# Weight parts and FFN activations in slots 4160 bytes apart instead of 4096

## The chip, the cores and the metric

The kernel runs on one core of a Trainium2 chip. The metric is the device time of one execution in microseconds (us). TensorE (PE, with its weight loads shown as PEld), VectorE (DVE), ScalarE (ACT), GpSimd (POOL) and SyncE (SP, which issues the DMAs) run side by side and wait for each other through semaphores.

## The reference

Two layers of a decoder trunk over 512 tokens of width 1024. Each layer has three sublayers, and each ends in a residual sum and a layer norm:

```python
for l in range(2):
    h = layer_norm(ALPHA * h + 0.5 * swiglu(h, ffn1_in[l], ffn1_out[l]), ...)   # D_FF = 2816
    mix = hybrid_mixer(h, ...)   # h @ w_in -> pooling, sparse attention, S5 -> @ w_out
    h = layer_norm(ALPHA * h + mix, ...)
    h = layer_norm(ALPHA * h + 0.5 * swiglu(h, ffn2_in[l], ffn2_out[l]), ...)

def swiglu(x, w_in, w_out):
    gate, up = jnp.split(x @ w_in, 2, axis=-1)
    return (jax.nn.silu(gate) * up) @ w_out
```

Four FFNs (two in each layer) hold most of the work; the two mixers stand between them.

## The kernel before

**Numbers in two parts.** A float32 operand of the large products is cut into a high part (`hi`, rounded to fp32r by ACT, L100) and a low part (`lo`, the rest, made by DVE, L101). A product is then three fp32r matmuls into the same PSUM bank: high by high, high by low and low by high (`mm3`, L247 to L249, and `project`, L395).

**Weights as units.** All weights stream from HBM as units of 128 partitions by 1024 float32 (4096 bytes in a partition), in the order in which PE wants them (`weight_units`). `Weights.load` issues the DMA of a unit into one of three staging slots `st`; `Weights.prep` takes the next unit, makes its parts `wh` and `wl` and issues further loads. The parts have six slots each in the pool `wsplit`; `done` gives slots back and `pump` fills them again. PE works through its units in a fixed order, ACT, DVE and SP work ahead of it.

**An FFN.** In the first half 44 units are used as the stationary operand: for each of 8 pieces `k` of the contraction PE loads 128 columns of `wh` or `wl` and streams 512 columns of `xh` or `xl`, the parts of the transposed input (names `g` and `u` in rows; `hd` for the first four units, which are done in two halves of 256 tokens). Silu and the product with `u` go to tiles `a`, two to a slot of the pool `act` (13 slots, tag `u`). In the second half 22 units are the moving operand: PE loads 128 columns of the activation's parts `ap` (in the same `act` slots) and streams 512 columns of `wh` or `wl` (name `o`, L395). The last four units of this half are put into `act` slots instead of `wsplit` (`W.alt`), so that all tokens of one tile can be finished together while the norm starts (`tail_and_head`).

**A mixer.** Its input projection streams weights past 128-token pieces of `xh` and `xl` (names `a`, `b`, `c`, `s`; of the `c` units a piece is 280 columns, or 1120 bytes, wide). Its output projection is like an FFN's second half, with `xh` and `xl` as stationary operand; its last four units (89 to 92 in the first layer) go to a pool `tail` of eight slots at the upper end of SBUF.

Each matmul of these lines has a weight load of its own. While one matmul runs, the load of the next one is under way.

Of the kernel before, what the change touches and what calls it, by code (L numbers as in the profile page):

```python
# [7 lines left out]
F32 = mybir.dt.float32  # L8
F32R = mybir.dt.float32r
# [20 lines left out]
PI2_A = 6.28125  # L30
PI2_B = 0.0019340515136718750
PI2_C = 1.2556659146363256e-06
CH = 4
NCH = SEQ // CH

# [20 lines left out]
class Weights:  # L56
# [23 lines left out]
    def prep(self):  # L80
        nc, i = self.nc, self.n_ready
        ap, n, raw = self.units[i]
        if raw:
            self.load(i + 6)
            t = self.split.tile([128, 1024], F32, tag="wh", name=f"wh{i}")
            nc.sync.dma_start(t[:, :n], ap)
            self.live.add(i)
            self.ready[i] = t
            self.n_ready += 1
            return  # L90
        self.load(i + 1)
        t = self.loaded.pop(i)
        if i in self.alt:
            pool, th, tl = self.alt[i], "u", "u"
        else:
            pool, th, tl = self.split, "wh", "wl"
            self.live.add(i)
        hi = pool.tile([128, 1024], F32R, tag=th, name=f"wh{i}")
        lo = pool.tile([128, 1024], F32R, tag=tl, name=f"wl{i}")
        nc.scalar.activation(hi[:, :n], t[:, :n], AF.Copy)  # L100
        nc.vector.tensor_tensor(lo[:, :n], t[:, :n], hi[:, :n].bitcast(F32), op=ALU.subtract)  # L101
        self.ready[i] = (hi, lo)
        self.n_ready += 1
        self.load(i + 4)
# [22 lines left out]
class Trunk:  # L127
# [65 lines left out]
    def start(self):  # L193

        nc, io, W = self.nc, self.io, self.W
        st = [W.stage.tile([128, 1024], F32, tag="st", name=f"st{u}") for u in range(2)]
        hi = [W.split.tile([128, 1024], F32R, tag="wh", name=f"wh{u}") for u in range(2)]
        lo = [W.split.tile([128, 1024], F32R, tag="wl", name=f"wl{u}") for u in range(2)]

        def parts(h, l, src):  # L200
            nc.scalar.activation(h, src, AF.Copy)  # L201
            nc.vector.tensor_tensor(l, src, h.bitcast(F32), op=ALU.subtract)  # L202

        with self.tc.tile_pool(name="x_in", bufs=8) as xp:
            warm = xp.tile([128, SEQ], mybir.dt.bfloat16, name="warm", bufs=1)
            nc.vector.memset(warm, 0.0)
            ps = self.bank("warm")
            for _ in range(WARM):
                nc.tensor.matmul(ps, lhsT=warm[:, :128], rhs=warm, start=True, stop=True)
            ts = [xp.tile([128, SEQ], F32, tag="xt", name=f"xt{k}") for k in range(KD)]  # L210

            def piece(u, c, run):
                if run:
                    parts(hi[u][:, c], lo[u][:, c], st[u][:, c])
                else:
                    nc.sync.dma_start(st[u][:, c], W.units[u][0][:, c])

            def column(k, run):
                if run:
                    parts(self.xh[:, k], self.xl[:, k], ts[k])  # L220
                else:
                    nc.sync.dma_start(ts[k], io["xT"][k])

            a, b = slice(0, 256), slice(256, 1024)
            for run in (False, True):
                piece(0, a, run)
                column(0, run)
                piece(1, a, run)
                column(1, run)
                piece(0, b, run)  # L230
                column(2, run)
                piece(1, b, run)
                for k in range(3, KD):
                    column(k, run)
                if not run:
                    W.n_loaded = 2
                    W.load(3)
        for u in range(2):
            W.ready[u] = (hi[u], lo[u])
            W.live.add(u)  # L240
        W.n_ready = 2
        nc.gpsimd.memset(self.expo, -0.5)
        nc.gpsimd.memset(self.bd, 0.0)

    def mm3(self, out, ah, al, bh, bl, start, stop):
        mm = self.nc.tensor.matmul
        mm(out, lhsT=ah, rhs=bh, start=start, stop=False)  # L247
        mm(out, lhsT=ah, rhs=bl, start=False, stop=False)  # L248
        mm(out, lhsT=al, rhs=bh, start=False, stop=stop)  # L249
# [258 lines left out]
    def s5_matrices(self, l, ap):  # L508
# [13 lines left out]
        def cmul(outr, outi, xr, xi, yr, yi, t):  # L522
            po.tensor_tensor(outr, xr, yr, op=ALU.mult)
            po.tensor_tensor(t, xi, yi, op=ALU.mult)
            po.tensor_tensor(outr, outr, t, op=ALU.subtract)
            po.tensor_tensor(outi, xr, yi, op=ALU.mult)
            po.tensor_tensor(t, xi, yr, op=ALU.mult)
            po.tensor_tensor(outi, outi, t, op=ALU.add)
# [8 lines left out]
        def wide(a):  # L537
            return a.unsqueeze(2).unsqueeze(3).to_broadcast([128, 8, 2, 16])
# [6 lines left out]
        def sub(m, s):  # L545
            return m.rearrange("p j (g s c) -> p j g s c", g=2, s=CH)[:, :, :, s]

        for s in range(CH - 1):
            k = CH - 1 - s
            cmul(sub(ebr, s), sub(ebi, s), br, bi, wide(prm[f"a{k}r"]), wide(prm[f"a{k}i"]), t)  # L550
        po.tensor_copy(sub(ebr, CH - 1), br)
        po.tensor_copy(sub(ebi, CH - 1), bi)
        cmul(fcr, fci, cr, ci, wide(prm["fr"]), wide(prm["fi"]), t)
# [47 lines left out]
    def s5_params(self, ap):  # L601
# [16 lines left out]
        def ts(a, s1, op0, s2=None, op1=None, out=None):  # L618
            out = tmp() if out is None else out
            if op1 is None:  # L620
                ve.tensor_scalar(out, a, s1, None, op0=op0)
            else:
                ve.tensor_scalar(out, a, s1, s2, op0=op0, op1=op1)
            return out

        def stt(a, s, b, op0, op1, out=None):
            out = tmp() if out is None else out
            ve.scalar_tensor_tensor(out, a, s, b, op0=op0, op1=op1)
            return out
# [12 lines left out]
        r = stt(n, -PI2_B, r, ALU.mult, ALU.add)  # L642
        r = stt(n, -PI2_C, r, ALU.mult, ALU.add)
        r = ts(r, 3.1415925, ALU.min, -3.1415925, ALU.max)
# [782 lines left out]
```

## Time and profile before

| | |
|---|---|
| median of 3 runs (lowest, highest) | 1978.22 us (1977.77, 1979.16) |
| the profiled execution, its own time | 1978.67 us |
| its span in the trace | 1976.9 us |
| PE busy | 1959.7 us, 99% of the span |
| DVE, ACT, POOL busy | 47%, 33%, 15% of the span |

The span runs from the first to the last instruction; 1.8 us of the execution's own time lie around it. A matmul's row shows its start and its length with the way through the array (0.39 us for 512 columns). Successive matmuls overlap, so the rate is read from the distance between starts, called a step here: first start to last start of a stretch, divided by the number of matmuls between them.

### The profile page before, as it was taken

To read this page: it belongs to the slowest core of one execution; us is meant where nothing else is said; L and a number is where in the kernel's file an instruction comes from. 1 tells how busy PE (TensorE), PEld (TensorE's weight loads), DVE (VectorE), ACT (ScalarE), POOL (GpSimd) and SP (SyncE) were. 2 spreads that over 40 slices of the span, in tenths; PEclk is the share of its full clock that TensorE was granted. 3 is DMA by queue.
4 is the path that set the end of the run, shared out by engine and by line. 5 is a ranking of instruction groups with operands and counts; after the bars stand their busy time and mean duration, and the time that the engine had idled before them with its cause. 6 is when DMAs were issued, how large, how long until landed. Compare 5 with 4: busy or idle time off the path is not lost.

```text
span 1976.9 us, 24780 instructions
## 1 busy us (share of the span) xinstructions
PE 1959.7 (99%) x9940; PEld 1643.0 (83%) x9940; DVE 920.4 (47%) x1434; ACT 648.4 (33%) x1144; POOL 288.5 (15%) x399
## 2 busy tenths in 40 slices
PE   9999999999999999999999999999999999999998
PEld 7888888898788888888898888888977898888886
DVE  5322333657976323233643223346779662223335
ACT  4222233135861222233222222331358622222320
POOL 1804000113321000000044220001223210000001
PEclk9999999999999999999999999999999999999999
DMA  8333334022111333334233333340211213223331
GB/s 286 111 95 90 105 97 139 20 79 75 54 64 66 117 96 96 96 96 127 76 113 101 92 96 96 96 139 9 90 64 44 87 63 107 96 96 96 96 96 43
DMA packets 57186, 183.21 MB, mean 93 GB/s; under 512 B 11248, under 2 KB 12016, under 8 KB 57072
## 3 DMA queue, kind: packets, MB, share of 16 engines
q1 hardware_dynamic: 57072, 181.64, 29.1%
q8 instruction: 78, 1.28, 0.3%
q14 instruction: 36, 0.29, 0.1%
HBM read 179.19 MB, written 2.10 MB: 92 GB/s over the span
## 4 chain that ended last, share of the span: by engine, by line
PE 95%; DVE 3%; ACT 1%; DMA 1%; issue 0%; POOL 0%; SPq 0%; DVEq 0%; ACTq 0%
PE o L395 28%; PE g L247 8%; PE g L248 8%; PE g L249 8%; PE u L247 8%; PE u L249 7%; PE u L248 7%; PE o L1079 2%; PE pt L1063 2%; PE hd L247 1%; PE hd L249 1%; PE hd L248 1%; PE hid L751 1%; PE tx L318 1%; PE s L1027 1%; PE s L248 1%
## 5 line engine op out<-in xcount | busy, mean ns | idle before, releaser
L101 DVE TENSOR_TENSOR wl<-st,wh 128x1024 fp32r<-128x1024 f32 x308 | 379.3, 1236 | 596.3 <-ACT wh L100 581.3
L100 ACT ACTIVATE wh<-st 128x1024 fp32r<-128x1024 f32 x308 | 323.8, 1055 | 923.2 <-PE g L248 351.8
L395 PE MATMUL o<-wh,ap 128*128 128x512 f32 x1408 | 379.2, 389 | 0.0
L395 PEld LDWEIGHTS o<-wh,ap 128*128 128x128 f32 x1408 | 263.8, 188 | 54.4
L247 PE MATMUL g<-xh,wh 128*128 128x512 f32 x656 | 256.7, 391 | 0.7 <-ACT xh L201 0.7
L248 PE MATMUL g<-xl,wh 128*128 128x512 f32 x656 | 255.6, 390 | 0.8 <-DVE xl L202 0.8
L249 PE MATMUL g<-xh,wl 128*128 128x512 f32 x656 | 255.4, 389 | 0.0
L247 PE MATMUL u<-xh,wh 128*128 128x512 f32 x656 | 255.2, 389 | 0.0
L248 PE MATMUL u<-xl,wh 128*128 128x512 f32 x656 | 255.2, 389 | 0.0
L249 PE MATMUL u<-xh,wl 128*128 128x512 f32 x656 | 255.2, 389 | 0.0
L395 PE MATMUL o<-wl,ap 128*128 128x512 f32 x704 | 217.4, 389 | 0.0
L287 POOL TENSOR_TENSOR mv<-mv,expo 128x1 f32<-128x1 f32 x24 | 35.6, 1485 | 1191.3 <-DVE mv L286 1191.3
L430 DVE TENSOR_TENSOR a<-a,u 128x512 f32<-128x512 f32 x82 | 56.4, 688 | 257.3 <-PE u L249 257.3
L395 PEld LDWEIGHTS o<-wl,ap 128*128 128x128 f32 x704 | 132.1, 188 | 27.6
L247 PEld LDWEIGHTS g<-xh,wh 128*128 128x128 f32 x656 | 123.2, 188 | 27.5 <-ACT xh L201 2.5
L248 PEld LDWEIGHTS g<-xl,wh 128*128 128x128 f32 x656 | 123.2, 188 | 26.8 <-DVE xl L202 1.7
L249 PEld LDWEIGHTS u<-xh,wl 128*128 128x128 f32 x656 | 123.2, 188 | 25.7
L249 PEld LDWEIGHTS g<-xh,wl 128*128 128x128 f32 x656 | 123.1, 188 | 25.7
L247 PEld LDWEIGHTS u<-xh,wh 128*128 128x128 f32 x656 | 123.1, 188 | 25.5
L248 PEld LDWEIGHTS u<-xl,wh 128*128 128x128 f32 x656 | 123.1, 188 | 25.6
L475 DVE TENSOR_TENSOR ap<-a,ap 128x512 fp32r<-128x512 f32 x88 | 60.3, 689 | 70.3 <-ACT ap L474 70.3
L474 ACT ACTIVATE ap<-a 128x512 fp32r<-128x512 f32 x88 | 54.5, 624 | 97.1 <-PE o L395 61.5
(348 smaller groups left out, 2604.1 us busy)
## 6 DMA issues: line engine op xcount, KB each, us to landing
st<-in_ffn_in SPq DMA_DIRECT2D x174, 512.0 KB, 3.5
st<-in_ffn_out SPq DMA_DIRECT2D x88, 512.0 KB, 3.5
st<-in_w_out SPq DMA_DIRECT2D x16, 512.0 KB, 3.5
st<-in_w_b SPq DMA_DIRECT2D x8, 512.0 KB, 4.3
st<-in_w_a SPq DMA_DIRECT2D x8, 512.0 KB, 3.6
ln_g<-in_ln_g SPq DMA_DIRECT2D x6, 512.0 KB, 4.0
ln_b<-in_ln_b SPq DMA_DIRECT2D x6, 512.0 KB, 5.0
xt<-in_xT SPq DMA_DIRECT2D x8, 256.0 KB, 6.5
```

Source lines behind the costliest of these rows:

```text
L100: nc.scalar.activation(hi[:, :n], t[:, :n], AF.Copy)
L101: nc.vector.tensor_tensor(lo[:, :n], t[:, :n], hi[:, :n].bitcast(F32), op=ALU.subtract)
L247: mm(out, lhsT=ah, rhs=bh, start=start, stop=False)
L248: mm(out, lhsT=ah, rhs=bl, start=False, stop=False)
L249: mm(out, lhsT=al, rhs=bh, start=False, stop=stop)
L287: nc.gpsimd.tensor_tensor(mv[:, 2:3], mv[:, 2:3], self.expo, op=ALU.pow)
L395: mm(ps[t][f], lhsT=a[:, q], rhs=w[:, 512 * f:512 * f + 512], start=(k == first and a is ah and w is wh), stop=end)
L430: nc.vector.tensor_tensor(a, a, u, op=ALU.mult)
L474: nc.scalar.activation(p[:, 0], a, AF.Copy)
L475: nc.vector.tensor_tensor(p[:, 1], a, p[:, 0].bitcast(F32), op=ALU.subtract)
L1063: nc.tensor.transpose(ps[:, 128 * k:128 * k + 128], p[:, i, 128 * k:128 * k + 128], ident)
L1079: mm(o[64 * i:64 * i + 64], lhsT=self.v[:, b, k, 64 * g:64 * g + 64], rhs=pt[:, i, 128 * k:128 * k + 128], start=False, stop=b == 1 and k ...
```

## The change

The tiles of the weights' parts are declared 1040 columns wide, of which the first 1024 are used. A slot of the pool is as wide as its widest tile, so all slots of tag `u` in `act` (with the activations `a` and their parts `ap`) and in `tail` grow too. No instruction is added, taken out or moved.

```diff
+W_SLOT = 1040
@@ Weights.prep
-            t = self.split.tile([128, 1024], F32, tag="wh", name=f"wh{i}")
+            t = self.split.tile([128, W_SLOT], F32, tag="wh", name=f"wh{i}")[:, :1024]
...
-        hi = pool.tile([128, 1024], F32R, tag=th, name=f"wh{i}")
-        lo = pool.tile([128, 1024], F32R, tag=tl, name=f"wl{i}")
+        hi = pool.tile([128, W_SLOT], F32R, tag=th, name=f"wh{i}")[:, :1024]
+        lo = pool.tile([128, W_SLOT], F32R, tag=tl, name=f"wl{i}")[:, :1024]
@@ Trunk.start
-        hi = [W.split.tile([128, 1024], F32R, tag="wh", name=f"wh{u}") for u in range(2)]
-        lo = [W.split.tile([128, 1024], F32R, tag="wl", name=f"wl{u}") for u in range(2)]
+        hi = [W.split.tile([128, W_SLOT], F32R, tag="wh", name=f"wh{u}")[:, :1024] for u in range(2)]
+        lo = [W.split.tile([128, W_SLOT], F32R, tag="wl", name=f"wl{u}")[:, :1024] for u in range(2)]
```

Where the slots lie in a partition, in bytes, as the built programs place them:

| slots | before: first, step | remainder modulo 512 | after: first, step | remainders modulo 512 |
|---|---|---|---|---|
| `xh`, `xl`, staging `st` | 17664, 34048, 61696 | 256 | the same | 256 |
| `wh`, six | 73984, 4096 | 256 | 73984, 4160 | 256, 320, 384, 448, 0, 64 |
| `wl`, six | 98560, 4096 | 256 | 98944, 4160 | 128, 192, 256, 320, 384, 448 |
| `act`, thirteen | 125184, 4096 | 256 | 125952, 4160 | 0, 64, 128 and so on, all eight |
| `tail` of the mixers, eight | 196576, 4096 | 480 | 196064, 4160 | 480, 32, 96 and so on, all odd multiples of 32 |

A piece of 128 or 512 columns inside a unit starts at a multiple of 512 bytes from the slot's start, so it has the slot's remainder. The program has 7872 matmuls on lines L247 to L249 and L395. In 7415 of the 7871 pairs of neighbours, before, the moving operand of one and the weights of the next (which are loaded meanwhile) start at the same remainder; after, in 1165 pairs, and the rest is spread over the other multiples of 64, with some 600 to 1100 pairs for each.

The order of the instructions is the same on every engine. Since pools are larger, some tiles lie over other earlier tiles than before, and seven instructions wait for other semaphores. On DVE, these are the subtractions that make the low parts of the mixer's last units in the first layer (89 to 92) and of the next FFN's first (93); before:

```order
L1085 TENSOR_TENSOR xl_74<-o221_4671,xh_73 128x4x128 [waits Activation_49]
L101 TENSOR_TENSOR wl89_4922<-st89_4489,wh89_4921 128x1024 [waits DMAHW7_49,Activation_49]
L101 TENSOR_TENSOR wl90_4928<-st90_4532,wh90_4927 128x1024 [waits DMAHW0_49,Activation_49]
L101 TENSOR_TENSOR wl91_4958<-st91_4574,wh91_4957 128x1024 [waits DMAHW1_49,Activation_49,Pool_49]
L101 TENSOR_TENSOR wl92_4964<-st92_4925,wh92_4963 128x1024 [waits DMAHW5_49,Activation_49]
L101 TENSOR_TENSOR wl93_4994<-st93_4931,wh93_4993 128x1024 [waits DMAHW6_49,Activation_49]
```

and with the change:

```order
L1086 TENSOR_TENSOR xl_74<-o221_4671,xh_73 128x4x128 [waits Activation_49]
L102 TENSOR_TENSOR wl89_4922<-st89_4489,wh89_4921 128x1024 [waits DMAHW7_49,Activation_49]
L102 TENSOR_TENSOR wl90_4928<-st90_4532,wh90_4927 128x1024 [waits DMAHW0_49,Activation_49,Pool_49]
L102 TENSOR_TENSOR wl91_4958<-st91_4574,wh91_4957 128x1024 [waits DVE_49,DMAHW1_49,Activation_49,Pool_49]
L102 TENSOR_TENSOR wl92_4964<-st92_4925,wh92_4963 128x1024 [waits DMAHW5_49,Activation_49]
L102 TENSOR_TENSOR wl93_4994<-st93_4931,wh93_4993 128x1024 [waits DMAHW6_49,Activation_49]
```

The rows and their order are the same (line numbers are one higher); units 90 and 91 wait for POOL and DVE, whose last writes of the attention's tiles lay where the slots now lie. The same two units of the second layer, and ACT's `wh` of unit 91 and its twin, change in this way too, and a copy to `tabc` on POOL in the second layer loses its waits.

## Rows read from the trace of the kernel before

**Rows 1.** The page: span, busy time and share of each engine, granted clock in 40 slices

```profile
span 1976.9 us, 24780 instructions
PE 1959.7 (99%) x9940; PEld 1643.0 (83%) x9940; DVE 920.4 (47%) x1434; ACT 648.4 (33%) x1144; POOL 288.5 (15%) x399
PEclk9999999999999999999999999999999999999999
```

**Rows 2.** The page: the chain that ended last, by engine

```profile
PE 95%; DVE 3%; ACT 1%; DMA 1%; issue 0%; POOL 0%; SPq 0%; DVEq 0%; ACTq 0%
```

**Rows 3.** The chain of waits, 253 to 368 us: start us, us, what

```profile
252.97 114.24 PE o L395 x504
```

**Rows 4.** Timeline of PE, an FFN's first half: start us, us, instruction

```profile
199.76 0.39 PE L247 MATMUL g<-xh,wh 128*128 128x512 f32 x1
...
204.52 0.39 PE L247 MATMUL u<-xh,wh 128*128 128x512 f32 x1
```

**Rows 5.** Timeline of PE, matmuls of 256 columns

```profile
623.78 0.28 PE L247 MATMUL hd<-xh,wh 128*128 128x256 f32 x1
...
626.18 0.28 PE L249 MATMUL hd<-xh,wl 128*128 128x256 f32 x1
```

**Rows 6.** Timeline of PE where the granted clock is low

```profile
1442.11 0.63 PE L247 MATMUL a<-wh,xh 128*128 128x512 f32 x1
...
1444.24 0.63 PE L249 MATMUL a<-wh,xl 128*128 128x512 f32 x1
```

**Rows 7.** Two stages: us, busy us of PE, PEld, DVE, ACT, POOL, clock, DMA

```profile
598.93:615.73 16.80, 16.80 (x73) 13.48 (x72) 11.42 (x17) 1.06 (x1) 3.06 (x2) 1.00 0.14 45
1442.11:1444.67 2.56, 2.56 (x8) 1.98 (x7) 1.72 (x3) 0.60 (x3) 0.00 (x0) 0.50 0.68 237
```

**Rows 8.** Timeline of PE, a mixer's output projection, units 89 on

```profile
598.93 0.63 PE L395 MATMUL o<-wh,xh 128*128 128x512 f32 x2
...
615.26 0.63 PE L395 MATMUL o<-wh,xl 128*128 128x512 f32 x2
615.73 1.03 PE L318 MATMUL tx<-cst,h 128*128 128x128 f32 x8
```

**Rows 9.** Timeline of PE, the `c` units, 280 columns, moving operand at three remainders

```profile
437.92 0.29 PE L247 MATMUL c<-wh,xh 128*128 128x280 f32 x1
...
438.30 0.29 PE L247 MATMUL c<-wh,xh 128*128 128x280 f32 x1
...
438.69 0.29 PE L247 MATMUL c<-wh,xh 128*128 128x280 f32 x1
...
439.07 0.29 PE L247 MATMUL c<-wh,xh 128*128 128x280 f32 x1
...
441.02 0.29 PE L247 MATMUL c<-wh,xh 128*128 128x280 f32 x1
```

**Rows 10.** Timeline of PE after a pause for transposes, the mixer's `b` units

```profile
380.83 0.39 PE L248 MATMUL b<-wl,xh 128*128 128x512 f32 x1
...
381.99 0.39 PE L247 MATMUL b<-wh,xh 128*128 128x512 f32 x1
...
382.67 0.39 PE L247 MATMUL b<-wh,xh 128*128 128x512 f32 x1
```

**Rows 11.** Timelines of POOL, DVE and ACT where attention ends and units 89 to 92 are made

```profile
572.24 1.04 POOL L1052 TENSOR_TENSOR p<-p,sum 128x512 f32<-128x512 f32 x1
571.46 0.66 DVE L1049 TENSOR_SCALAR p<-p,sum,gt 128x512 f32<-128x512 f32 x1
577.61 2.95 ACT L100 ACTIVATE wh<-st 128x1024 fp32r<-128x1024 f32 x3
578.69 3.50 DVE L101 TENSOR_TENSOR wl<-st,wh 128x1024 fp32r<-128x1024 f32 x3 [0.26 <-ACT wh L100]
```

**Rows 12.** Tile `wl`, 560 to 600 us: duration ns min/median/max

```profile
L101 DVE TENSOR_TENSOR wl<-st,wh x9: 1219/1226/1226, 578.7 to 595.2; 128x1024 fp32r<-128x1024 f32 x9
```

**Rows 13.** The page's costliest group: busy us, mean ns, idle before and its releaser

```profile
L101 DVE TENSOR_TENSOR wl<-st,wh 128x1024 fp32r<-128x1024 f32 x308 | 379.3, 1236 | 596.3 <-ACT wh L100 581.3
```

## The prediction

> **What bounds the kernel now.** I read the page's first and second part, then the chain of waits, then PE's timeline in the stretches that make up most of the span. PE is busy for 1959.7 of 1976.9 us and has the full clock in every slice [rows 1], and the chain that ended last lies on PE for 95% [rows 2]; DVE, next in line, is busy for 47%. So the time is the number of matmuls times the distance between their starts (the step), and a change can only pay or cost here if it changes the step or makes PE wait.
>
> The step is the same wherever weights are used in an FFN. In a second half 504 matmuls of 512 columns take 114.24 us, 226.7 ns each [rows 3]; in a first half, where the weights are the stationary operand, 21 steps take 204.52 - 199.76 = 4.76 us, again 226.7 ns [rows 4]. At 2.4 GHz, the clock's upper level, 512 columns are 213.3 ns of array time, so 13.3 ns come on top. Matmuls of 256 columns show what sort of surplus it is: 20 steps in 2.40 us, 120.0 ns [rows 5], which is 106.7 + 13.3. It is a sum per matmul, not a rate. Where the clock was granted at half (1.2 GHz), five steps take 2.13 us, 426 ns [rows 6, 7]: 512 columns alone are 426.7 there, and the surplus is gone. So it isn't something that the array does in its own cycles; the matmul seems to be held up by what feeds it, its own stream from SBUF and the load of the next weights, which runs meanwhile. This is the only place at which an address could count.
>
> **The change part by part.**
>
> *Instructions and order.* None is added or moved: 0.
>
> *Waits.* Units 90 and 91 wait for POOL and DVE too. What they wait for are the attention's last writes of `p`, which end on POOL at 572.24 + 1.04 = 573.28 us and on DVE at 572.12; the first of the conversions concerned starts on ACT at 577.61 and on DVE at 578.69 [rows 11]. The release is 4.3 us ahead of ACT and 5.4 us ahead of DVE, and behind these rows stand only conversions, whose parts PE wants from 598.93 us on [rows 8]. Cost 0. Without that slack each us of delay would first use up the time to 598.93.
>
> *ACT, DVE and DMA.* They write and read the moved slots. The nine subtractions from 578.7 to 595.2 us go to slots at remainder 480 (units 89 to 92) and 256 (the next FFN's) and all take 1219 to 1226 ns [rows 12], so I expect no change in their length. If there were one, DVE has idle time before 308 such instructions of 596.3 us in total, nearly 2 us each [rows 13]. Cost 0, and covered by that idle time.
>
> *The matmuls.* 7872 matmuls use weights. In 7415 - 1165 = 6250 pairs of neighbours the stream and the load that runs beside it no longer start at one remainder. All of the gain or loss lies in what the step is then. Three rows bear on it.
>
> First, alignment by itself. In a mixer's output projection the units 89 to 92 lie at remainder 480, an odd multiple of 32, and 72 matmuls take 16.80 us, 233.3 ns each [rows 7, 8]: 6.7 ns more than at remainder 256, with the clock full and the same columns. 6.7 ns are 16 columns, and 16 columns of 4 bytes are 64 bytes. A stream of 2048 bytes that starts at an odd multiple of 32 touches 33 pieces of 64 bytes instead of 32; I read the surplus as that piece. By this reading every slot of `wsplit` and `act` after the change, all at multiples of 64, is as good as 256, and the mixers' `tail` slots, still at odd multiples of 32, stay at 233: no change in either.
>
> Second, the distance between stream and load. In those 72 matmuls the two are 224 bytes apart modulo 512, and after the extra piece of 6.7 ns the surplus over the array's time is 13.3 ns as at distance 0. In the mixer's `c` units the load is always at 256 while the stream starts at 256, 352 and 448 in turn, three matmuls each: they take 0.38, 0.39 and 0.38 us, and all 24 take 3.10 us, 129.2 ns each [rows 9]. 280 columns and 13.3 ns would be 130.0. Distances 96 and 192 thus cost nothing that can be seen, and save 0.8 ns at most, which over 6250 matmuls is 5 us.
>
> Third, a row that speaks the other way. After a pause for transposes the first matmuls, all at distance 0, need 232 ns (five steps in 1.16 us) before they settle at 226.7 (three in 0.68 us) [rows 10]. So the step does depend on how stream and load stand to each other in time.
>
> The bounds are: no surplus left, 6250 x -13.3 ns = -83 us, since the half-clock row shows that the surplus can vanish; and the worst steady step in the trace, 6250 x 6.7 ns = +42 us. I take 0, because the rows at other distances (96, 192, 224) are the nearest to what the change makes, and they show the surplus unchanged. The Trainium skill ("TensorE: Matmul & The Clock Gate", Part 2, the step on LDWEIGHTS) says that PE has two independent read ports and that loading the next weights takes no read bandwidth from the running matmul. By it the placement is worth nothing; the `c` units agree, the 232 ns after a pause do not fit it quite, so it raises the chance of no change only a little.
>
> *Sum.* 0 + 0 + 0 + 0 on the profiled execution's 1978.67 us (span 1976.9 and 1.8 around it). The median of the runs is 0.45 us lower, so I forecast 1978.3 us for the median.
>
> **The rivals.**
>
> *Out of step, slower.* Inside a unit the loads alternate `wh`, `wh`, `wl`, which now lie at different remainders, and the settled step of 226.7 might never be reached. Place: all FFN matmuls. Price: 232 - 226.7 = 5.3 ns x 6250 = +33 us, 2011 us; with the worst step 2020. It decides from 4 us / 6250 = 0.63 ns on. For it: [rows 10]. Against it: the `c` units change their remainder every three matmuls and don't get slower by it.
>
> *One remainder is the collision, faster.* Stream and load start together at the same remainder in nearly every pair; if that causes the surplus, spreading them saves it. Sparing one piece of 64 bytes gives 6250 x 6.7 = -42 us, 1937 us; all of it 1895; the `c` units' 0.8 ns gives 1973. For it: the surplus vanishes at the half clock. Against it: at distance 224 it is all there. By the formula of the Trainium skill (the same page, "Back-to-back issue gap") a warm matmul of 512 columns is 215.8 ns behind the next; that would be 10.9 x 6250 = 68 us less, an estimate from the page of 1911 us. No steady row here comes near 215.8.
>
> *The placement does nothing to PE.* Then the time is the forecast's, for another reason: the 233.3 ns at remainder 480 would have to come from something else in that stage.
>
> **How the numbers follow.** What a measurement of this kernel can tell from no change is about 0.2%, 4 us (the three runs spread over 1.4 us). No change, by pieces of 64 bytes or because placement does nothing: 0.52. Slower, out of step: 0.24, of which a third above 2010. Faster: 0.24, about half of it only a few us up to 28 us, the other half below 1950. The range from 1950 to 2010 leaves out some 0.08 above and 0.12 below. The likeliest case's own range is 1974 to 1982.
>
> **What would show it.** Right: 504 matmuls of an FFN's second half still take 114.2 us, g and u steps stay at 226.7 ns, units 89 to 92 at 233, conversions at 1226 ns, no new wait at 578 us. Wrong: a step in the FFNs that differs from 226.7 by more than 0.6 ns, above all one that differs from unit to unit as the remainders go round; this alone would make the prediction wrong, and its sign tells which rival holds. If only second halves move, it is the stream's own remainder; if first halves move too, it is the distance to the load.

## The result, and the profile after

| | before | with the change |
|---|---|---|
| median of 4 runs (lowest, highest) | 1978.3 us (1977.77, 1979.16) | 2005.35 us (2005.26, 2005.43) |
| ratio, 95% interval | | 1.0136 (1.0119 to 1.0154) |
| span of the profiled execution | 1976.9 us | 2003.5 us |

The kernel is 27 us slower. The page of the changed kernel, first and second part:

```profile
span 2003.5 us, 24781 instructions
PE 1987.1 (99%) x9940; PEld 1642.4 (82%) x9940; DVE 918.6 (46%) x1434; ACT 648.3 (32%) x1144; POOL 288.5 (14%) x399
PEclk9999999999999999999999999999999999999999
```

Against [rows 1] PE is busy for 27.4 us more with the same number of matmuls, under the same clock, while DVE, ACT and POOL do the same work in the same time. So the matmuls themselves have become slower. The stretch of an FFN's second half in the chain of waits, which was 114.24 us [rows 3]:

```profile
258.14 116.46 PE o L396 x504
```

231.1 ns each in place of 226.7. Two starts in a first half (timeline of PE: start us, us, instruction), where 15 steps lie between the rows:

```profile
202.24 0.39 PE L248 MATMUL g<-xh,wh 128*128 128x512 f32 x1
...
205.72 0.39 PE L248 MATMUL g<-xh,wh 128*128 128x512 f32 x1
```

That is 232.0 ns where [rows 4] had 226.7. Summed over all starts of the two traces, by what the matmul belongs to:

| matmuls | number | change of the sum of their steps | for each |
|---|---|---|---|
| first halves of the FFNs (`g`, `u`) | 3936 | +20.0 us | +5.1 ns |
| second halves (`o` with `ap`) | 2112 | +9.0 us | +4.3 ns |
| `hd`, 256 columns | 576 | -1.4 us | -2.4 ns |
| the mixers' `a` | 192 | -2.0 us | |
| everything else | | +1.3 us | |
| all | | +26.9 us | |

At least half of the gain in `a` comes from the clock. The matmuls that ran at the half clock in [rows 6], five steps in 2.13 us, have the full clock in this trace (the view by windows: us, busy us of PE, PEld, DVE, ACT, POOL, clock, DMA; then the same matmuls in the timeline of PE):

```profile
1458.60:1485.00 26.40, 25.05 (x167) 21.88 (x166) 16.64 (x29) 13.43 (x33) 2.93 (x2) 1.00 0.37 120
1462.86 0.39 PE L248 MATMUL a<-wh,xh 128*128 128x512 f32 x1
...
1464.01 0.40 PE L250 MATMUL a<-wh,xl 128*128 128x512 f32 x1
```

The five steps take 1.15 us here, 1.0 us less. Whether the change spared that stretch or chance did, these two traces don't tell.

The new waits cost nothing. The timelines of POOL, ACT and DVE at the place of [rows 11, 12] (start us, us, instruction):

```profile
579.65 1.04 POOL L1053 TENSOR_TENSOR p<-p,sum 128x512 f32<-128x512 f32 x1
585.02 2.94 ACT L101 ACTIVATE wh<-st 128x1024 fp32r<-128x1024 f32 x3
586.11 3.50 DVE L102 TENSOR_TENSOR wl<-st,wh 128x1024 fp32r<-128x1024 f32 x3 [0.26 <-ACT wh L101]
```

And the tile view of `wl` in the same stretch (count, then shortest, median and longest ns):

```profile
L102 DVE TENSOR_TENSOR wl<-st,wh x10: 1216/1224/1226, 586.1 to 608.0; 128x1024 fp32r<-128x1024 f32 x10
```

POOL is done at 580.69 us, 4.3 us ahead of ACT's first conversion and 5.4 ahead of DVE's, and these ten subtractions still take 1216 to 1226 ns, at whatever remainder their slots lie.

### The profile page after: what moved, and what is told of

The parts are those of the page before. It is cut to its first block, busy times and chain, and to the rows that moved or that the text cites. A ratio compares the mean times of both kernels' runs of the same rounds, so it can differ in the third digit from the quotient of the medians.

```text
span 2003.5 us, 24781 instructions
## 1 busy us (share of the span) xinstructions
PE 1987.1 (99%) x9940; PEld 1642.4 (82%) x9940; DVE 918.6 (46%) x1434; ACT 648.3 (32%) x1144; POOL 288.5 (14%) x399
## 4 chain that ended last, share of the span: by engine, by line
PE 95%; DVE 3%; issue 1%; ACT 1%; POOL 0%; DMA 0%; SPq 0%; DVEq 0%; ACTq 0%
PE o L396 28%; PE u L250 8%; PE g L249 8%; PE g L250 8%; PE g L248 8%; PE u L249 8%; PE u L248 8%; PE o L1080 2%; PE pt L1064 1%; PE hd L249 1%; PE hd L248 1%; PE hd L250 1%; PE hid L752 1%; PE tx L319 1%; PE s L1028 1%; PE s L249 1%
## 5 line engine op out<-in xcount | busy, mean ns | idle before, releaser
L396 PE MATMUL o<-wh,ap 128*128 128x512 f32 x1408 | 384.8, 393 | 0.0
L249 PE MATMUL g<-xl,wh 128*128 128x512 f32 x656 | 258.6, 394 | 0.8 <-DVE xl L203 0.8
L249 PE MATMUL u<-xl,wh 128*128 128x512 f32 x656 | 258.4, 394 | 0.0
L249 PEld LDWEIGHTS g<-xl,wh 128*128 128x128 f32 x656 | 123.2, 188 | 29.9 <-DVE xl L203 1.4
L249 PEld LDWEIGHTS u<-xl,wh 128*128 128x128 f32 x656 | 123.3, 188 | 29.1
```

The source lines that it names most:

```text
L396: mm(ps[t][f], lhsT=a[:, q], rhs=w[:, 512 * f:512 * f + 512], start=(k == first and a is ah and w is wh), stop=end)
```

## The experiments

Three theories could explain a slower step. **A**: it depends on the distance between the address where a stream starts and the one where the load beside it starts. **B** (the rival of the prediction): a unit's loads alternate between remainders and the step never settles. **C**: stream or load must start at certain remainders by itself.

### Shifts with slots 4096 apart

`shift_weights_64` moves weights and activations by 64 bytes against `xh` and `xl`; `shift_all_64` and `shift_all_32` move all of them together.

```diff
 # shift_weights_64: a tile of 64 bytes ahead of the slots
+        self.gap = ctx.enter_context(tc.tile_pool(name="gap", bufs=1))
+        nc.gpsimd.memset(self.gap.tile([128, 16], F32, name="gap"), 0.0)
         self.wpool = ctx.enter_context(tc.tile_pool(name="wsplit", bufs=self.slots))
 # shift_all_64 (and with 8 columns shift_all_32): a tile ahead of xh
+        nc.gpsimd.memset(self.const.tile([128, 16], F32, name="gap"), 0.0)
         self.xh = self.const.tile([128, KD, SEQ], F32R, name="xh")
```

> Slots of weights and activations stay 4096 apart but all start 64 bytes later (remainder 320 modulo 512); xh and xl stay at 256. So in an FFN's first half the load of wh or wl starts 64 after the stream, always by the same distance, and in its second half stream and load start at one remainder again. Theory A (the step depends on the distance between the stream's start and the start of the load that runs beside it): first halves at about 233 ns, as units with both parts at 320 have in the changed kernel, second halves at 226.7; about 4000 matmuls x 6.7 ns, near 2004 us. Theory B (the loads of a unit alternate between remainders and never settle): nothing alternates, 226.7 everywhere, 1978 us. Theory C (a stream or load must itself start at 256 or 0 modulo 512): both halves slower, near 2018 us.

> Everything from xh on starts 64 bytes later: xh, xl, weights and activations all at remainder 320, slots 4096 apart. Theory A (distance): distance 0 as before, 226.7 ns everywhere, 1978 us. Theory B (alternation): 1978 us. Theory C (own remainder of stream or load): all FFN matmuls slower, near 2018 us.

> Everything from xh on starts 32 bytes later: xh, xl, weights and activations all at remainder 288, an odd multiple of 32, at distance 0 from each other. If a stream that starts at an odd multiple of 32 pays for one more piece of 64 bytes, as the prediction read the 233.3 ns at remainder 480, all steps go to 233.3 and the time to about 1978 + 6250 x 6.7 ns = 2020 us. If it was the distance of 224 in that stage that cost (theory A), the time stays at 1978 us.

Here and further on, the ratio is to runs of the kernel before that were made beside each experiment; their medians were 1977.34 us for these three, and 1978.59 and 1977.81 us for the later ones.

| run | median us | ratio to before (95%) | change of `g`, `u` | change of second halves |
|---|---|---|---|---|
| shift_weights_64 | 2001.8 | 1.0123 (1.0108 to 1.0138) | +25.4 us | +0.3 us |
| shift_all_64 | 1978.21 | 1.0004 (0.9995 to 1.0013) | +0.1 us | 0.0 us |
| shift_all_32 | 1978.74 | 1.0006 (0.9996 to 1.0016) | +0.1 us | +0.1 us |

In `shift_weights_64` an FFN's first half, nine steps of PE's timeline:

```profile
203.03 0.40 PE L249 MATMUL g<-xh,wh 128*128 128x512 f32 x1
...
205.13 0.39 PE L249 MATMUL g<-xh,wh 128*128 128x512 f32 x1
```

And its second half in the chain of waits:

```profile
259.19 114.28 PE o L397 x504
```

233.3 ns in the first half, 226.7 in the second, where stream and load start at one remainder. This is theory A as it was written down. Theory B is out as the sole cause, since nothing alternates here. Theory C is out too: with all at 320, or all at 288, the time is that of before. `shift_all_32` also fells a reading of the prediction: every stream of the FFNs starts at an odd multiple of 32 and pays nothing. Its second half in the chain of waits:

```profile
252.71 114.25 PE o L396 x504
```

### Steps by themselves

`steps_alone` has nothing but matmuls in the pattern of a first half, in groups of 48 with chosen remainders:

```python
for name, m, h, l, n in sets():     # remainders of the streams, of wh, of wl; columns
    for r in range(2):
        for k in range(8):
            mm(ps[:, :n], lhsT=u, rhs=a, ...)   # wh with xh
            mm(ps[:, :n], lhsT=u, rhs=b, ...)   # wh with xl
            mm(ps[:, :n], lhsT=v, rhs=a, ...)   # wl with xh
```

> Only matmuls, all else left out (the output is a constant): groups of 48 in the pattern of an FFN's first half (wh with xh, wh with xl, wl with xh), without any other engine at work. load_a to load_p: stream at 256, both loads at 256 + 0, 32, ... 480. both_a to both_p: stream and loads together at 0, 32, ... 480. move_a to move_p: loads at 256, stream at 256 + 0, 32, ... 480. alt_a to alt_h: stream and wh at 256, wl at 256 + 0, 64, ... 448. half_a to half_h: 256 columns, loads at 256 + 0, 64, ... 448. Theory A: load_ and move_ vary with the distance (226.7 at 0, about 233 at +64, 229 to 233 at others), both_ is flat at 226.7. Theory B: only alt_ is slow. Theory C: both_ varies. If 64-byte pieces count: the odd letters' neighbours at odd multiples of 32 in both_ (both_b, both_d, ...) stand at 233.3 and the others at 226.7.

Starts of the 24th and the 48th matmul of five groups (timeline of PE), 24 steps apart:

```profile
21.92 0.39 PE L57 MATMUL load_a<-mh,wl 128*128 128x512 f32 x1
...
27.36 0.40 PE L57 MATMUL load_a<-mh,wl 128*128 128x512 f32 x1
...
44.16 0.39 PE L57 MATMUL load_c<-mh,wl 128*128 128x512 f32 x1
...
49.76 0.39 PE L57 MATMUL load_c<-mh,wl 128*128 128x512 f32 x1
...
88.86 0.39 PE L57 MATMUL load_g<-mh,wl 128*128 128x512 f32 x1
...
94.35 0.39 PE L57 MATMUL load_g<-mh,wl 128*128 128x512 f32 x1
...
221.88 0.39 PE L57 MATMUL both_c<-mh,wl 128*128 128x512 f32 x1
...
227.32 0.40 PE L57 MATMUL both_c<-mh,wl 128*128 128x512 f32 x1
...
644.51 0.28 PE L57 MATMUL half_b<-mh,wl 128*128 128x256 f32 x1
...
647.34 0.28 PE L57 MATMUL half_b<-mh,wl 128*128 128x256 f32 x1
```

226.7 ns with load and streams at 256; 233.3 with the loads 64 further on; 228.8 with 192; 226.7 again with both at 64; 117.9 for 256 columns with the loads 64 on. All groups in that way, last 24 steps (from starts in whole ns, where the rows above are rounded to 10):

| load ahead of stream, bytes | 0 | 32 | 64 | 96 | 128 | 160 | 192 | 224 |
|---|---|---|---|---|---|---|---|---|
| `load_`, 512 columns, ns | 226.7 | 233.3 | 233.3 | 234.5 | 232.7 | 233.3 | 228.9 | 233.3 |
| the same plus 256 bytes | 226.7 | 233.3 | 233.3 | 234.4 | 232.7 | 233.3 | 228.9 | 233.3 |
| `half_`, 256 columns | 120.0 | | 117.8 | | 118.7 | | 117.8 | |

All sixteen `both_` groups stand at 226.6 to 226.7: as long as the distance stays the same from matmul to matmul, it alone counts, and modulo 256. `move_`, with the streams shifted, gives 226.7 at 0 and 256 and 228.9 to 234.2 elsewhere. `alt_`, with `wl` alone off by 64, 128 or 192, gives 231.1: more than the 227.4 to 228.9 that a mean over the pairs at each distance would be. Either alternation costs something of its own, as B has it, or it is too simple to count for each stream only the load of the next matmul. And while these steps run no other engine is at work, so PE alone, with the address of its loads, is enough to bring the effect about.

### The parts of the change, and another pitch

```diff
 # pitch_256
-W_SLOT = 1040
+W_SLOT = 1088
 # weights_only: the units in act and tail keep 1024 columns (in prep; hi and lo)
-        hi = pool.tile([128, W_SLOT], ...)
+        hi = pool.tile([128, W_SLOT if pool is self.split else 1024], ...)
 # activations_only: the other way round, and 1024 in start and for raw units
+        hi = pool.tile([128, 1024 if pool is self.split else W_SLOT], ...)
```

For the expectations each of the 6827 pairs of neighbours with 512 columns was given the step of its distance from the table; for the whole change that makes 24.8 us against before.

> The change with slots 4352 bytes apart (1088 columns) in place of 4160: remainders 0 and 256 modulo 512. The loads of a unit and the streams still change their remainder from slot to slot, and pools are larger still. If only the distance modulo 256 counts (as load_a and load_i of steps_alone show, 226.67 both), every pair in the FFNs is at distance 0 and the time is that of before, 1978 us. If the distance counts modulo 512, or larger slots or a change of slot cost by themselves, it is slower: up to the 2005 us of the change.

> Only the slots of wsplit 4160 apart; activations, their parts and the units in act and tail 4096 apart as before. Distances after: first halves as in the change, second halves with streams at 0, 64, 128, 192 modulo 256 and loads at 0. Summed over the program with the steps of steps_alone by distance: +22.8 us against before, 2001 us. If the two parts of the change matter by number of moved operands alone (4032 of 6144 in the first halves), about +18 us.

> Only the slots of act (activations, their parts, the last four units of an FFN) and tail 4160 apart; wsplit as before. First halves stay at 226.67; in second halves the loads go to 0, 64, 128, 192 modulo 256 while most streams stay at 0. By the steps of steps_alone +7.0 us against before, 1985 us. If the two parts simply added up, it would be 27.0 less what weights_only adds.

| run | median us | ratio to before (95%) | change of `g`, `u` | change of second halves | all steps |
|---|---|---|---|---|---|
| pitch_256 | 1978.18 | 0.9997 (0.9987 to 1.0006) | -0.3 us | 0.0 us | -0.1 us |
| weights_only | 2005.32 | 1.0130 (1.0113 to 1.0147) | +21.9 us | +7.5 us | +27.4 us |
| activations_only | 1984.07 | 1.0028 (1.0019 to 1.0037) | +0.2 us | +7.3 us | +5.5 us |

The second half of the first FFN in the chain of waits of `pitch_256`:

```profile
252.24 114.24 PE o L396 x504
```

The same of `weights_only`:

```profile
260.20 116.05 PE o L396 x504
```

And of `activations_only`:

```profile
253.05 116.27 PE o L396 x504
```

`pitch_256` grows the slots four times as much as the change, its streams and loads change slots in the same way, and no cost can be seen: larger pools, new overlaps and a change of slot are free within the interval, and a distance of 256 bytes is as good as 0. The two parts don't add up (27.4 + 5.5 against 26.9): each alone takes second halves off distance 0, by 7.5 and 7.3 us, and both together cost only 9.0, since either puts the same pairs at a distance and the second merely exchanges one distance for another. The table's estimate of 22.8 for `weights_only` is below the measured 27.4: steps of groups with one constant distance don't describe loads that alternate. For `activations_only` the estimate of 7.0 is met by the second halves' 7.3; the sum of all steps is only 5.5 because `a` takes 1.5 us less, and this trace too has the full clock where [rows 6] had half. Why `g` and `u` differ by 1.8 us between `weights_only` and the whole change is open.

### Whose load, finer distances, and the tail

`steps_alone_2` has finer distances, one stream off, and a second half's pattern. `steps_alone_3` takes two remainders in turn, so that either a matmul's own load or the load beside its stream is at distance 0, and has bfloat16 groups. `tail_aligned` moves the pools at the upper end of SBUF:

```diff
+        self.top = ctx.enter_context(tc.tile_pool(name="top", bufs=1, side="right"))
+        nc.gpsimd.memset(self.top.tile([128, 56], F32, name="top"), 0.0)
         self.const = ctx.enter_context(tc.tile_pool(name="const", bufs=1))
```

> Only matmuls again, the rest left out. fine_: both loads 4, 8, 12, 16, 20, 24, 28, 36, 48 bytes behind the stream's remainder. low_: only the second stream (xl) off by 32, 64, ... 224. pair_: xl and wl off together. out_: pattern of a second half (each load for two streams), loads off by 0, 32, ... 224. turn_: wh off by +32 j, wl by -32 j. If the memory is read in pieces of 32 bytes and only equal pieces run in step, fine_a to fine_g lie between 226.7 and 233.3 or at one of the two; if some distance spares the 13.3 ns, a step under 226.7 shows here and would be a placement better than before. out_ should follow load_ of the first run: 226.7, 233.3, 233.3, 234.4, 232.7, 233.3, 228.9, 233.3.

> Only matmuls, the rest left out. Two remainders taken in turn, 256 and 256 + 0, 32, ... 224. own_: each matmul's load and stream start at the same remainder, so the load that runs beside a stream (that of the next matmul) is off by plus or minus the distance. beside_: each stream starts where the next matmul's load does, its own load is off. If it is the load running beside the stream that counts, beside_ is flat at 226.67 and own_ shows 229 to 235 except at 0; if it is a matmul's own load, the other way round. bf_: bfloat16 streams and loads, both loads off by 0, 32, ... 224; half the bytes for each column, so if the bytes that the stream wants in each ns are what leaves no room, bf_ shows no difference.

> The kernel before with the pools at the upper end of SBUF moved down by 224 bytes, so that the tail slots of the mixers (units 89 to 92 and their twins) start at remainder 256 instead of 480, as xh and xl do. If the distance sets the step, the stage from 598.93 to 615.73 us takes 72 x 226.67 = 16.3 us instead of 16.8, and the same in its rest and in the second mixer: 192 x 6.7 ns = 1.3 us in all, 1977 us, too little for the times to show but plain in the trace. If something else in that stage costs the 6.7 ns (the norms beside it, a piece more), the step stays at 233.3.

Distances of 4 to 28 bytes (`fine_`) give 230.0 to 235.0 ns, so being in the same piece of 32 bytes doesn't help; the second half's pattern (`out_`) repeats the table within 0.6 ns. `turn_`, where `wh` and `wl` are off in opposite directions, gives 228.9 to 232.1; with 192 and 64 it takes 228.9, where a mean over the pairs at each distance would be 230.4. So that mean is too low for `alt_` and too high here. One stream off (`low_`) or `xl` and `wl` off together (`pair_`) gives 228.9 to 233.3. No group of fp32r with 512 columns settles below 226.67: the placement of before is the best that was found.

From `steps_alone_3`, 24 steps each:

```profile
43.45 0.39 PE L55 MATMUL own_c<-ml,wl 128*128 128x512 f32 x1
...
49.01 0.39 PE L55 MATMUL own_c<-ml,wl 128*128 128x512 f32 x1
...
132.26 0.39 PE L55 MATMUL beside_c<-ml,wl 128*128 128x512 f32 x1
...
137.82 0.39 PE L55 MATMUL beside_c<-ml,wl 128*128 128x512 f32 x1
```

Both take 231.7 ns. Over all distances but 0, `own_` has 228.3 to 234.0 and `beside_` 230.0 to 231.7. Neither is flat: I had expected one of them to be. Which load it is that a stream collides with isn't settled by this; it may reach over two streams. With that, it stays open too whether alternation has a price of its own. The bfloat16 groups take 215.8 ns at every distance. Two of them in the timeline of PE (of the 48 matmuls of each the trace has 47), from whose starts 10.36 us follow for 48 steps:

```profile
203.72 10.52 PE L55 MATMUL bf_b<-bm,bw 128*128 128x512 bf16 x47
214.08 10.52 PE L55 MATMUL bf_c<-bm,bw 128*128 128x512 bf16 x47
```

They differ from the fp32r groups in the load as well, which takes 98 ns in place of 188 (tile views of `own_c` and `bw`: shortest, median and longest ns):

```profile
L55 PEld LDWEIGHTS own_c<-mh,wh x24: 187/188/188, 37.9 to 48.5; 128*128 128x128 f32 x24
L55 PEld LDWEIGHTS <-bw x384: 96/98/101, 193.3 to 275.8; 128*128 128x128 bf16 x192
```

`tail_aligned`, the stage of [rows 8] in the timeline of PE:

```profile
598.46 0.62 PE L397 MATMUL o<-wh,xh 128*128 128x512 f32 x2
...
614.79 1.03 PE L320 MATMUL tx<-cst,h 128*128 128x128 f32 x8
```

72 steps in 16.33 us, 226.8 ns in place of 233.3, with the same norms beside them. The mixers' output projections lose 1.2 us. The whole kernel has a median of 1976.93 us, ratio 0.9994 (0.9985 to 1.0003): the stage is faster, but the time can't be told from that of before.

## Why the forecast of no change failed

The prediction's parts on instructions, waits, ACT and DVE held, with the slack of 4.3 and 5.4 us that it had read. The case forecast as likeliest, 1974 to 1982 us, didn't come: the term put at 0 for the matmuls measured 27 us. That 2005.35 us still lies between 1950 and 2010 is owed to the width which the rivals gave that range, not to the mechanism that was forecast; by the prediction's own sign, an FFN step more than 0.6 ns off 226.7, that mechanism was wrong. Its last sign held: first halves moved too, so it is the distance to the load. It failed in the part on the matmuls, at its first and second point.

*"First, alignment by itself"*: the 6.7 ns more at remainder 480 were read as one more piece of 64 bytes. `shift_all_32` puts every stream at such a remainder at no cost, and `tail_aligned` removes the 6.7 ns by removing the distance. [Rows 7, 8] were the one stage of the trace before that already ran off distance 0 for long, and showed the price of it: load minus stream is 32 modulo 256 there, and the table has 233.3 for 32. The sum of a column count and 64 bytes fitted by chance.

*"Second, the distance"*: having taken the piece off, the prediction found the same surplus at distance 224 as at 0 and concluded that distance was free; that followed from the first error. Its other witness, the `c` units at 129.2 ns, could not bear witness: with 256 columns the settled steps are 117.8 to 120.0 ns and the longest of them is that at distance 0 (`half_`). A short matmul doesn't pay what one of 512 columns pays, so nothing could be carried over from 280 columns. In the changed kernel `hd` became faster by 2.4 ns each, and the `c` units themselves take 131.3 ns a step where they had 131.6 before (184 steps each).

*"Third, a row that speaks the other way"* was the right one. The rival built on it, out of step, had the sign and the place. Its price of 5.3 ns for each of 6250 pairs, 33 us, was taken from a step that had not settled; measured were 5.1 ns on 3936 and 4.3 ns on 2112 matmuls, less 1.4 us in `hd` and 2.0 us in `a`, of which the clock gave at least 1.0, and 27 us in all. That 5.3 comes near 5.1 is luck, since the 232 ns after a pause stood at distance 0; what made them no run here tells. Its mechanism, loads that alternate, isn't needed: a constant distance alone costs 6.7 ns (`shift_weights_64`). Whether alternation adds to it is open (`alt_`, `turn_`).

The other rival, faster by avoiding a collision at one remainder, had the sign wrong for matmuls of 512 columns: starting at one remainder modulo 256 is the cheapest relation of all that ran.

The rule that PE's two read ports don't disturb each other (the Trainium skill, "TensorE: Matmul & The Clock Gate", Part 2, the step on LDWEIGHTS) had raised the chance of no change a little. Here the runs differ from it: with fp32r at the full clock and no other engine at work, the step goes from 226.7 to 234.5 ns by the address of the load alone. With bfloat16 they agree: 215.8 ns at every distance. The formula N / 2.4 + 2.5 of the Trainium skill (the same page, "Back-to-back issue gap", where it stands for the gap of an isolated matmul) gives the same 215.8 ns for 512 columns.

That the array wants twice the bytes per column in fp32r, and so leaves the load too little room at the full clock, fits the bfloat16 groups and the half clock of [rows 6], where the surplus is gone. It is argued, not shown: in the bfloat16 groups the load is shorter too (98 ns), and why 256 columns are slowest at distance 0 isn't explained by it. What in SBUF repeats every 256 bytes no run here tells.

## What to carry to other kernels

Where dense fp32r matmuls of 512 columns, each with a load of its own, bound a kernel, let the start of the moving operand and of the stationary operand be equal modulo 256 bytes in a partition, in all slots: the pool pitches of 4096 and 4352 bytes, both multiples of 256, kept it, and padding a slot by 64 bytes lost 2% in such a stage (231.1 to 232.0 ns for 226.7). Before carrying a step from one stage to another, look whether the stage has the same number of columns: what binds 512 columns may not bind 256. And a stage that is slower for an unexplained reason (233.3 ns here) deserves one test of each reason before one of them goes into a sum.

## What the runs showed of the hardware that was not expected

- The step of fp32r matmuls of 512 columns depends on the distance modulo 256 bytes between stream and load. Where it is constant: 226.7 ns at 0, 228.9 at 192, 232.7 to 234.5 at the other multiples of 32; 4 bytes off already costs 5.7 ns (`fine_a`, 232.3).
- Absolute remainders, odd multiples of 32 included, cost nothing (sixteen `both_` groups, 226.6 to 226.7).
- With 256 columns distance 0 is the slowest (120.0 ns against 117.8 and 118.7 at the other multiples of 64), the other way round.
- bfloat16 shows none of it: 215.8 ns in all eight groups, with loads of 98 ns in place of 188.
